# Pinning the VectorE and ScalarE order of a trunk's last projection, and moving two weight tiles and a low-rank half

## The chip, the cores and the metric

One core of one Trainium2 chip runs the whole program. The time is the device time of one execution in microseconds (us). A program of this kind has five engines that run their own instruction lists in parallel (TensorE, VectorE, ScalarE, GpSimd and SyncE, in the profile PE, DVE, ACT, POOL and SP) and wait for each other by semaphores. Most transfers here are issued by SP.

## The reference, cut to what matters

Two layers of a streaming encoder run over 4096 prompt frames and 32 sample frames of width 1024. Layer 0 splits one input projection into a convolution branch and a gated linear recurrence; layer 1 pools trailing frames. Each layer adds its gated output to the stream, and a final RMSNorm follows:

```python
        h = rms_norm(x, norm_g[l]) * (1.0 + scale[:, None, :]) + shift[:, None, :]
        if l % 2 == 0:
            y, cb, gs = even_mixer(h, ...)
        else:
            y, pb = pool_mixer(h, ...)
        x = x + gate[:, None, :] * y
    return rms_norm(x, final_g), ...
```

Two pieces of it matter here. In `even_mixer` the value columns v and 16 low-rank columns lr come out of the same projection, and the forget gate is made from lr: `log_a = log_sigmoid(lr @ gate_w2 + gate_b) / 16`. In `pool_mixer` the last line is the last projection, `(p * scale * silu(gate)) @ w_out`, a product of 4128 rows by 1024 with a 1024 by 1024 matrix.

## The kernel before, in words

All products are float32 products in three passes: each operand is split into a high and a low part, and high by high, high by low and low by high are summed in PSUM. ScalarE writes the high part of an operand, VectorE subtracts it from the source and writes the low part. For a weight tile `split_w` does this (lines 116 to 119), one ScalarE and one VectorE instruction of 128x1024 per tile, from a staging buffer into which SP has loaded it. There are two such staging buffers (tag `st`), so the load of a tile waits for the split of the tile two before it.

The rows go in 11 blocks, ten of 384 rows and a last one of 256 prompt and 32 sample rows, through these stages:

- Stage A makes the convolution branch's projections, stage C the first layer's output projection, stage D the second layer's input projection and pooling. They are touched by the change only through `split_w`, which issues the same instructions there.
- Stage B, the recurrence branch (lines 874 to 1020). Its loop over blocks interleaves the projection of the block at hand with the attention of the block before. A tile of 128 rows makes its v and lr columns in two halves (`v_unit`, line 874, PSUM names `psv`): half 0 is 264 columns of v, half 1 the other 248 and the 16 lr columns (`lrt`). When all tiles are done, VectorE splits lr (`lrs`, lines 930 and 932), TensorE transposes it (`pslr`, line 936), ScalarE evacuates it (`lrT`), TensorE makes the first gate column tile (`psg`) and then the forget gate (`psz`). The attention pieces of the block before are the calls pa, pk, pu, po and pt: scores (`psat`), key transposes and state update (`psku`), output (`pso`), and the transposes of the normalized output (`psoT`, from `on`, line 845). The last block also loads and splits eight weight tiles of stage C (`w_c`).
- Stage E, the last projection (from line 1327). It takes the prompt rows in 16 pairs of 128-row tiles. A pair is a 2 by 2 block product done with Strassen's and Winograd's seven products. The left operands are the quarters y of two tiles and their combinations S1 to S4 (`comb`, line 1370); `make(i)` (lines 1373 to 1385) splits the operand of product i into `op`, ScalarE first, VectorE behind it. The right operands are 14 weight tiles, `w_e` 0 to 13, of which product i uses 2i and 2i+1. Each product is 12 matmuls of 128x512. The products go in turn into three PSUM banks, and after each one VectorE adds the bank to the residual rows `xE` (`add`, line 1441). Bank 0 serves products 0, 2, 4 and 6, so product 2 can't start before the add behind product 0 has read it, and so on. The rows of the first tile are complete after product 5, those of the second after product 6. Then `finish` (lines 1396 to 1404) squares and sums them on ScalarE (`junkE`), makes 1/rms on GpSimd in two instructions (`rt_E`, `rE`), scales on VectorE (`SCALAR_TENSOR_TENSOR`, line 1403) and stores the tile. `make(i)` for the next pair follows each add.
- Behind the 16 pairs come the sample rows with eight more weight tiles (`load_S`, `w_s` 0 to 7, split in the last pair) in two products `psES`, and their own norm.

The order of the work: a scheduler sets each engine's list, except where `tc.keep_in_program_order` ties an instruction to the source's order. In stages B to E only TensorE is tied (`PIN["on"]`). In stage E, VectorE, ScalarE and SP are in the scheduler's order. `load_E(0)` to `load_E(11)` stand in the last block of stage D (line 1322), `load_E(12)` and `load_E(13)` in stage E behind `make(3)` (line 1418).

Of the kernel before, what the change touches and what calls it, by code (L numbers as in the profile page):

```python
# [8 lines left out]
F32 = mybir.dt.float32  # L9
# [3 lines left out]
AF = mybir.ActivationFunctionType  # L13
ALU = mybir.AluOpType
# [16 lines left out]
def trunk(  # L31
# [8 lines left out]
    nc = tc.nc  # L40
# [8 lines left out]
    while L - s0 > TB - NS:  # L49
        b = Blk()  # L50
# [65 lines left out]
    def split_w(w, st, nk, n):  # L116

        nc.scalar.activation(w[:, 0], st, AF.Copy)  # L118
        nc.vector.tensor_tensor(out=w[:, 1], in0=st, in1=w[:, 0].bitcast(F32), op=ALU.subtract)  # L119

# [37 lines left out]
    PASS = ((0, 0), (0, 1), (1, 0))  # L158
    PIN = {"on": False, "act": False}

# [572 lines left out]
    with ExitStack() as bctx:  # L733
# [169 lines left out]
        for blk in blocks:  # L903
# [17 lines left out]
            v_unit(blk, hs, vt, lrt, 1, 1)  # L921
            pk(2), pt(0)
            v_unit(blk, hs, vt, lrt, 2, 0)
            pu(2), po(2)
            v_unit(blk, hs, vt, lrt, 2, 1)
            pt(1)

# [334 lines left out]
    with tc.tile_pool(name="D", bufs=2, reuse_waits="tile") as dp:  # L1262
# [3 lines left out]
        for blk in blocks:  # L1266
# [3 lines left out]
            for idx, (kind, j) in enumerate(dord):  # L1270
# [45 lines left out]
                if blk.last:  # L1316

                    if idx < 8:
                        rv_load(idx)
                    if 2 <= idx < 10:  # L1320
                        rv_gemm(idx - 2, hs)
                    if 1 <= idx < 13:
                        load_E(idx - 1, halves=idx <= 8)
# [3 lines left out]
    with tc.tile_pool(name="E", bufs=2, reuse_waits="tile") as ep:  # L1327
        PIN["on"] = True

# [30 lines left out]
        class Left:  # L1360
# [7 lines left out]
            def comb(self, out, a, b, op):  # L1368
                t = ep.tile([P, 4, P], F32, tag="S", name=f"{out}_{self.p}", bufs=4)
                nc.vector.tensor_tensor(out=t, in0=self.A[a], in1=self.A[b], op=op)  # L1370
                self.A[out] = t

            def make(self, i):
                if i == 2:
                    self.comb("S1", "A21", "A22", ALU.add)
                    self.comb("S2", "S1", "A11", ALU.subtract)
                if i == 4:
                    self.comb("S3", "A11", "A21", ALU.subtract)
                if i == 5:
                    self.comb("S4", "A12", "S2", ALU.subtract)  # L1380
                src = self.A[("A11", "A12", "S2", "S1", "S3", "S4", "A22")[i]]
                o = ep.tile([P, 2, 4, P], F32R, tag="op", name=f"op{self.p}_{i}", bufs=8)
                nc.scalar.activation(o[:, 0], src, AF.Copy)  # L1383
                nc.vector.tensor_tensor(out=o[:, 1], in0=src, in1=o[:, 0].bitcast(F32), op=ALU.subtract)  # L1384
                self.ops[i] = o
# [10 lines left out]
        def finish(xt, n, name, dst):  # L1396
            junk = ep.tile([P, D], BF16, tag="junk", name=f"junk{name}", bufs=1)
            ss = sm.tile([P, 1], F32, tag="ss", name=f"ss{name}")
            nc.scalar.activation(junk[:n], xt[:n], AF.Square, accum_out=ss[:n])
            r = sm.tile([P, 1], F32, tag="r", name=f"r{name}")  # L1400
            rstd_pool(r[:n], ss[:n], n, 1, 1.0 / D, name)
            yield
            nc.vector.scalar_tensor_tensor(out=xt[:n], in0=xt[:n], scalar=r[:n], in1=fg[:n], op0=ALU.mult, op1=ALU.mult)
            nc.sync.dma_start(dst, xt[:n])
# [10 lines left out]
        for i in range(7):  # L1415
            cur.make(i)
            if i == 3:
                load_E(12, ep), load_E(13, ep)
                nc.sync.dma_start(fg, final_g.partition_broadcast(P))
# [14 lines left out]
        for p in range(len(pairs)):  # L1434
# [5 lines left out]
            def add(x, h, ps):  # L1440
                nc.vector.tensor_tensor(out=x[:, H[h]], in0=ps, in1=x[:, H[h]], op=ALU.add)  # L1441

# [75 lines left out]
```

## Time and profile before

| what | value |
|---|---|
| runs | 2895.23, 2896.0 and 2900.14 us, median 2896.0 us |
| the profiled execution | 2898.6 us, its span 2896.9 us |
| mean clock granted to TensorE | 0.993 of full speed |
| TensorE busy | 2819.6 us, 97% of the span |
| VectorE busy | 1964.5 us, 68% |
| ScalarE busy | 1031.9 us, 36% |
| GpSimd busy | 243.8 us, 8% |

The span is the time between the first and the last recorded work of the core; the execution's own time is measured outside of it and is 1.7 us longer. Busy times are averages over stages with different limits, and a share of 97% says only that TensorE is the engine that nearly everything waits for: a microsecond can be won where TensorE stands still or runs at its lower clock.

### The profile page before, as it was taken

To read this page: it belongs to the slowest core of one execution; us is meant where nothing else is said; L and a number is where in the kernel's file an instruction comes from. 1 tells how busy PE (TensorE), PEld (TensorE's weight loads), DVE (VectorE), ACT (ScalarE), POOL (GpSimd) and SP (SyncE) were. 2 spreads that over 40 slices of the span, in tenths; PEclk is the share of its full clock that TensorE was granted. 3 is DMA by queue.
4 is the path that set the end of the run, shared out by engine and by line. 5 is a ranking of instruction groups with operands and counts; after the bars stand their busy time and mean duration, and the time that the engine had idled before them with its cause. 6 is when DMAs were issued, how large, how long until landed. Compare 5 with 4: busy or idle time off the path is not lost. (4 is left out here: it accounts for less than half of the span.)

```text
span 2896.9 us, 43268 instructions
## 1 busy us (share of the span) xinstructions
PE 2819.6 (97%) x16593; PEld 2613.4 (90%) x16593; DVE 1964.5 (68%) x3907; ACT 1031.9 (36%) x2137; POOL 243.8 (8%) x492
## 2 busy tenths in 40 slices
PE   7999999999999999998999999999999999999998
PEld 5999999998999999997878888999999999977776
DVE  4997886888788888885866675533333333587766
ACT  4434334334344333333232224422322322433333
POOL 1110000000000000001111110011111110000000
PEclk9999999999999999999999999999999999999999
DMA  8422322242211111115455554322222221464544
GB/s 287 155 86 104 110 104 91 79 120 75 61 52 45 45 51 59 38 55 173 164 197 184 194 196 139 112 68 71 70 69 68 71 68 51 150 205 147 167 145 145
DMA packets 249666, 323.69 MB, mean 112 GB/s; under 512 B 18793, under 2 KB 198907, under 8 KB 248947
## 3 DMA queue, kind: packets, MB, share of 16 engines
q1 hardware_dynamic: 248635, 318.78, 33.9%
q8 instruction: 130, 2.13, 0.3%
q0 software_dynamic: 704, 2.11, 0.2%
q14 instruction: 77, 0.63, 0.1%
q10 hardware_dynamic: 120, 0.04, 0.0%
HBM read 211.21 MB, written 109.65 MB: 111 GB/s over the span
## 5 line engine op out<-in xcount | busy, mean ns | idle before, releaser
L162 PE MATMUL psC<-w_c,hC 128*128 128x512 f32 (+1 forms) x1568 | 377.9, 398 | 0.0
L162 PE MATMUL psD<-h,w_du 128*128 128x384 f32 (+1 forms) x2112 | 376.6, 332 | 0.1
L162 PE MATMUL psD<-h,w_dg 128*128 128x384 f32 (+1 forms) x2112 | 376.4, 332 | 0.0
L413 DVE SCALAR_TENSOR_TENSOR co<-g,cwt,co 128x384 f32<-128x384 f32 (+1 forms) x660 | 370.1, 606 | 4.9
L162 PEld LDWEIGHTS psD<-h,w_du 128*128 128x128 f32 x2112 | 357.8, 188 | 0.9 <-DVE h L152 0.4
L162 PEld LDWEIGHTS psD<-h,w_dg 128*128 128x128 f32 x2112 | 357.8, 188 | 0.4
L162 PEld LDWEIGHTS psC<-w_c,hC 128*128 128x128 f32 (+1 forms) x1568 | 293.6, 190 | 60.8
L413 DVE SCALAR_TENSOR_TENSOR coB<-glB,cwt,coB 128x384 f32<-128x384 f32 x600 | 333.8, 614 | 0.0
L162 PE MATMUL psE<-w_e,op 128*128 128x512 f32 x1344 | 310.7, 392 | 18.5 <-DVE xE L1441 13.9
L162 PEld LDWEIGHTS psE<-w_e,op 128*128 128x128 f32 x1344 | 252.0, 189 | 77.1 <-ACT op L1383 21.6
L162 PE MATMUL psv<-w_wv,hB 128*128 128x264 f32 (+1 forms) x1568 | 207.8, 288 | 2.1 <-ACT vt L887 2.1
L162 PEld LDWEIGHTS psv<-w_wv,hB 128*128 128x128 f32 (+1 forms) x1568 | 194.9, 187 | 6.4 <-ACT vt L887 2.5
L162 PE MATMUL psA<-h,w_aglu 128*128 128x384 f32 (+1 forms) x1056 | 191.9, 335 | 0.4 <-ACT h L172 0.2
L162 PE MATMUL psg<-hB,w_bg 128*128 128x384 f32 (+1 forms) x1056 | 190.8, 338 | 1.4 <-DVE xn L708 1.4
L162 PE MATMUL psA<-h,w_aval 128*128 128x384 f32 (+1 forms) x1056 | 189.1, 333 | 0.0
L162 PE MATMUL psA<-h,w_agate 128*128 128x384 f32 (+1 forms) x1056 | 187.2, 333 | 0.0
L162 PEld LDWEIGHTS psg<-hB,w_bg 128*128 128x128 f32 x1056 | 182.7, 192 | 2.1 <-issue 1.6
L1290 DVE COPY halo<-u 128x15 f32<-128x15 f32 x80 | 14.2, 178 | 250.7 <-ACT u L1286 250.7
L162 PEld LDWEIGHTS psA<-h,w_aglu 128*128 128x128 f32 x1056 | 180.4, 189 | 2.8 <-issue 1.7
L162 PEld LDWEIGHTS psA<-h,w_aval 128*128 128x128 f32 x1056 | 178.4, 188 | 0.1
L162 PEld LDWEIGHTS psA<-h,w_agate 128*128 128x128 f32 x1056 | 178.0, 188 | 0.1
L1311 DVE SCALAR_TENSOR_TENSOR sgD<-p,gbs,sgD 128x384 f32<-128x384 f32 (+1 forms) x96 | 56.1, 591 | 125.4 <-ACT sgD L1307 124.0
(268 smaller groups left out, 3719.1 us busy)
## 6 DMA issues: line engine op xcount, KB each, us to landing
x<-in_x_prompt SPq DMA_DIRECT2D x64, 512.0 KB
aw<-in_ada_w SPq DMA_DIRECT2D x32, 512.0 KB
x1D<-x SPq DMA_DIRECT2D x32, 512.0 KB
x<-x1D SPq DMA_DIRECT2D x32, 512.0 KB
out<-xE SPq DMA_DIRECT2D x32, 512.0 KB
hfD<-hf_a SPq DMA_DIRECT2D x80, 192.0 KB
hfB<-hfD SPq DMA_DIRECT2D x40, 384.0 KB
y1D<-sgD SPq DMA_DIRECT2D x80, 192.0 KB
```

The costliest lines, as they stand in the source:

```text
L162: ins = nc.tensor.matmul(*args, **kw)
L413: nc.vector.scalar_tensor_tensor(out=out[:, :w], in0=src[:, j:j + w], scalar=cwt[:, c, j:j + 1], in1=out[:, :w], op0=ALU.mult, op1=ALU.add)
L1290: nc.vector.tensor_copy(halo[:, j, :], u[:, TB:TB + PP])
L1311: nc.vector.scalar_tensor_tensor(out=y1[:, c0:c0 + m], in0=pt[:, a:a + m], scalar=gbs[:, j:j + 1], in1=sgt[:, c0:c0 + m], op0=ALU.add, op1 ...
```

## The change

It has four parts. ScalarE's and VectorE's instructions of stage E are tied to the source's order, as TensorE's are: the splits, combinations, adds and the two ends of `finish`. `load_E(10)` and `load_E(11)` move from the last block of stage D to behind `make(1)` of the first pair in stage E. In stage B the third tile's half 1 (with the lr columns) is made before its half 0, and ahead of the state update `pu(2)` and the transposes `pt(0)`. Outside of stage E the new `pin` and `act` do nothing, as the flags are off there.

```diff
@@ -115,8 +115,8 @@
 
     def split_w(w, st, nk, n):
 
-        nc.scalar.activation(w[:, 0], st, AF.Copy)
-        nc.vector.tensor_tensor(out=w[:, 1], in0=st, in1=w[:, 0].bitcast(F32), op=ALU.subtract)
+        act(w[:, 0], st, AF.Copy)
+        pin(nc.vector.tensor_tensor(out=w[:, 1], in0=st, in1=w[:, 0].bitcast(F32), op=ALU.subtract))
 
     def wslot(name):
         return wp.tile([P, SLOT], F32R, tag="w", name=name)
@@ -156,7 +156,11 @@
         return h
 
     PASS = ((0, 0), (0, 1), (1, 0))
-    PIN = {"on": False, "act": False}
+    PIN = {"on": False, "act": False, "dve": False}
+
+    def pin(ins):
+        if PIN["dve"]:
+            tc.keep_in_program_order(ins)
 
     def mmul(*args, **kw):
         ins = nc.tensor.matmul(*args, **kw)
@@ -919,11 +923,11 @@
             v_unit(blk, hs, vt, lrt, 1, 0)
             pu(1), po(1), pa(2)
             v_unit(blk, hs, vt, lrt, 1, 1)
-            pk(2), pt(0)
+            pk(2)
+            v_unit(blk, hs, vt, lrt, 2, 1)
+            pu(2), pt(0)
             v_unit(blk, hs, vt, lrt, 2, 0)
-            pu(2), po(2)
-            v_unit(blk, hs, vt, lrt, 2, 1)
-            pt(1)
+            po(2), pt(1)
 
             lrs = bp.tile([P, 2 * P], F32R, tag="kA", name=f"lrs{blk.i}")[:, 0:144].rearrange("p (i a b) -> p i a b", i=3, a=3)
             for (i0, i1, m) in ([(0, nsub, P)] if not blk.last else [(i, i + 1, sb[1]) for i, sb in enumerate(blk.subs)]):
@@ -1319,13 +1323,13 @@
                         rv_load(idx)
                     if 2 <= idx < 10:
                         rv_gemm(idx - 2, hs)
-                    if 1 <= idx < 13:
+                    if 1 <= idx < 11:
                         load_E(idx - 1, halves=idx <= 8)
             hs = nxt
     hctx.close()
 
     with tc.tile_pool(name="E", bufs=2, reuse_waits="tile") as ep:
-        PIN["on"] = True
+        PIN["on"] = PIN["act"] = PIN["dve"] = True
 
         ep.tile([P, D], F32, tag="x", name="x_first", bufs=4)
         ep.tile([P, 2048], F32R, tag="we", name="we_first", bufs=2)
@@ -1367,7 +1371,7 @@
 
             def comb(self, out, a, b, op):
                 t = ep.tile([P, 4, P], F32, tag="S", name=f"{out}_{self.p}", bufs=4)
-                nc.vector.tensor_tensor(out=t, in0=self.A[a], in1=self.A[b], op=op)
+                pin(nc.vector.tensor_tensor(out=t, in0=self.A[a], in1=self.A[b], op=op))
                 self.A[out] = t
 
             def make(self, i):
@@ -1380,8 +1384,8 @@
                     self.comb("S4", "A12", "S2", ALU.subtract)
                 src = self.A[("A11", "A12", "S2", "S1", "S3", "S4", "A22")[i]]
                 o = ep.tile([P, 2, 4, P], F32R, tag="op", name=f"op{self.p}_{i}", bufs=8)
-                nc.scalar.activation(o[:, 0], src, AF.Copy)
-                nc.vector.tensor_tensor(out=o[:, 1], in0=src, in1=o[:, 0].bitcast(F32), op=ALU.subtract)
+                act(o[:, 0], src, AF.Copy)
+                pin(nc.vector.tensor_tensor(out=o[:, 1], in0=src, in1=o[:, 0].bitcast(F32), op=ALU.subtract))
                 self.ops[i] = o
 
         def prod(ps, left, i, first):
@@ -1396,11 +1400,11 @@
         def finish(xt, n, name, dst):
             junk = ep.tile([P, D], BF16, tag="junk", name=f"junk{name}", bufs=1)
             ss = sm.tile([P, 1], F32, tag="ss", name=f"ss{name}")
-            nc.scalar.activation(junk[:n], xt[:n], AF.Square, accum_out=ss[:n])
+            act(junk[:n], xt[:n], AF.Square, accum_out=ss[:n])
             r = sm.tile([P, 1], F32, tag="r", name=f"r{name}")
             rstd_pool(r[:n], ss[:n], n, 1, 1.0 / D, name)
             yield
-            nc.vector.scalar_tensor_tensor(out=xt[:n], in0=xt[:n], scalar=r[:n], in1=fg[:n], op0=ALU.mult, op1=ALU.mult)
+            pin(nc.vector.scalar_tensor_tensor(out=xt[:n], in0=xt[:n], scalar=r[:n], in1=fg[:n], op0=ALU.mult, op1=ALU.mult))
             nc.sync.dma_start(dst, xt[:n])
 
         ends = []
@@ -1414,6 +1418,8 @@
         cur, xs = Left(0), load_xE(0)
         for i in range(7):
             cur.make(i)
+            if i == 1:
+                load_E(10), load_E(11)
             if i == 3:
                 load_E(12, ep), load_E(13, ep)
                 nc.sync.dma_start(fg, final_g.partition_broadcast(P))
@@ -1438,7 +1444,7 @@
             bank = [mm([P, 512], f"psE{p}_{q}") for q in range(3)]
 
             def add(x, h, ps):
-                nc.vector.tensor_tensor(out=x[:, H[h]], in0=ps, in1=x[:, H[h]], op=ALU.add)
+                pin(nc.vector.tensor_tensor(out=x[:, H[h]], in0=ps, in1=x[:, H[h]], op=ALU.add))
 
 
             for i, (q, first, adds) in enumerate(((0, 1, (x1, 0)), (1, 1, (x1, 0)), (0, 0, (x1, 1)), (2, 1, (x2, 1)),
```

Where instructions moved, first on VectorE at the start of stage E, behind the last instruction of stage D. `w_e` are low parts of weight tiles, `op0_i` those of pair 0's operands (pair number, then product), `S1_0` to `S4_0` its combinations. Before:

```order
L119 TENSOR_TENSOR w_e12_25319<-st_e12_25320,w_e12_25319 128x1024
L119 TENSOR_TENSOR w_e13_25324<-st_e13_25325,w_e13_25324 128x1024
L1384 TENSOR_TENSOR op0_0_25303<-y0_0_25295,op0_0_25303 128x512
L1384 TENSOR_TENSOR op0_1_25306<-y0_0_25295,op0_1_25306 128x512
L1370 TENSOR_TENSOR S1_0_25309<-y0_1_25297 128x512
L1370 TENSOR_TENSOR S2_0_25311<-S1_0_25309,y0_0_25295 128x512
L1370 TENSOR_TENSOR S3_0_25330<-y0_0_25295,y0_1_25297 128x512
L1370 TENSOR_TENSOR S4_0_25335<-y0_0_25295,S2_0_25311 128x512
L1384 TENSOR_TENSOR op0_2_25313<-S2_0_25311,op0_2_25313 128x512
L1384 TENSOR_TENSOR op0_3_25316<-S1_0_25309,op0_3_25316 128x512
L1384 TENSOR_TENSOR op0_4_25332<-S3_0_25330,op0_4_25332 128x512
L1384 TENSOR_TENSOR op0_5_25337<-S4_0_25335,op0_5_25337 128x512
```

With the change:

```order
L1388 TENSOR_TENSOR op0_0_25293<-y0_0_25285,op0_0_25293 128x512
L1388 TENSOR_TENSOR op0_1_25296<-y0_0_25285,op0_1_25296 128x512
L119 TENSOR_TENSOR w_e10_25299<-st_e10_25300,w_e10_25299 128x1024
L119 TENSOR_TENSOR w_e11_25304<-st_e11_25305,w_e11_25304 128x1024
L1374 TENSOR_TENSOR S1_0_25309<-y0_1_25287 128x512
L1374 TENSOR_TENSOR S2_0_25311<-S1_0_25309,y0_0_25285 128x512
L1388 TENSOR_TENSOR op0_2_25313<-S2_0_25311,op0_2_25313 128x512
L1388 TENSOR_TENSOR op0_3_25316<-S1_0_25309,op0_3_25316 128x512
L119 TENSOR_TENSOR w_e12_25319<-st_e12_25320,w_e12_25319 128x1024
L119 TENSOR_TENSOR w_e13_25324<-st_e13_25325,w_e13_25324 128x1024
L1374 TENSOR_TENSOR S3_0_25330<-y0_0_25285,y0_1_25287 128x512
L1388 TENSOR_TENSOR op0_4_25332<-S3_0_25330,op0_4_25332 128x512
```

The splits of tiles 12 and 13 stood ahead of the first operands; now tiles 10 and 11 (that were split in stage D) stand behind the first two operands, tiles 12 and 13 behind the fourth, and S3 and S4 behind them.

VectorE again, in a pair in mid-stage, from the add behind product 5 of pair 3 (`xE3_0<-psE3_2`) on. The add into `xE3_1` is that behind product 6, the adds into `xE4_0` are the first two of pair 4. Before:

```order
L1441 TENSOR_TENSOR xE3_0_25643<-psE3_2_25798,xE3_0_25643 128x512
L1384 TENSOR_TENSOR op4_6_25934<-y4_1_25790,op4_6_25934 128x512
L1403 SCALAR_TENSOR_TENSOR xE3_0_25643<-xE3_0_25643,rE3_0_25903,fg_25292 128x1024
L1441 TENSOR_TENSOR xE3_1_25645<-psE3_0_25796,xE3_1_25645 128x512
L1384 TENSOR_TENSOR op5_0_25963<-y5_0_25937,op5_0_25963 128x512
L1403 SCALAR_TENSOR_TENSOR xE3_1_25645<-xE3_1_25645,rE3_1_25930,fg_25292 128x1024
L1441 TENSOR_TENSOR xE4_0_25792<-psE4_0_25945,xE4_0_25792 128x512
L1384 TENSOR_TENSOR op5_1_25979<-y5_0_25937,op5_1_25979 128x512
L1441 TENSOR_TENSOR xE4_0_25792<-psE4_1_25946,xE4_0_25792 128x512
```

With the change:

```order
L1447 TENSOR_TENSOR xE3_0_25643<-psE3_2_25798,xE3_0_25643 128x512
L1374 TENSOR_TENSOR S4_4_25907<-y4_0_25788,S2_4_25848 128x512
L1388 TENSOR_TENSOR op4_5_25909<-S4_4_25907,op4_5_25909 128x512
L1447 TENSOR_TENSOR xE3_1_25645<-psE3_0_25796,xE3_1_25645 128x512
L1407 SCALAR_TENSOR_TENSOR xE3_0_25643<-xE3_0_25643,rE3_0_25903,fg_25282 128x1024
L1388 TENSOR_TENSOR op4_6_25934<-y4_1_25790,op4_6_25934 128x512
L1447 TENSOR_TENSOR xE4_0_25792<-psE4_0_25945,xE4_0_25792 128x512
L1407 SCALAR_TENSOR_TENSOR xE3_1_25645<-xE3_1_25645,rE3_1_25930,fg_25282 128x1024
L1388 TENSOR_TENSOR op5_0_25963<-y5_0_25937,op5_0_25963 128x512
L1447 TENSOR_TENSOR xE4_0_25792<-psE4_1_25946,xE4_0_25792 128x512
L1388 TENSOR_TENSOR op5_1_25979<-y5_0_25937,op5_1_25979 128x512
```

The scale of a tile's rows now has one or two more instructions between it and the add whose sum it waits for, and S4 and the operand of product 5, which were made earlier, now follow the add behind product 5.

ScalarE in stage B, last block (`psv10_2x` is its third tile, x the half; `9_2` names pieces of the block before). Before:

```order
L783 ACTIVATE kA9_2_13615<-psku9_2_13612 128x256
L206 ACTIVATE vt10_2_13406<-psv10_20_13628 32x264
L838 ACTIVATE junkB9_2_13664,ss49_2_13663<-pso9_20_13653 128x128 x2
L838 ACTIVATE junkB9_2_13664,ss49_2_13663<-pso9_21_13654 128x128
L118 ACTIVATE w_c00_14281<-st_c00_14279 128x1024
L838 ACTIVATE junkB9_2_13664,ss49_2_13663<-pso9_21_13654 128x128
L118 ACTIVATE w_c01_14286<-st_c01_14284 128x1024
L206 ACTIVATE lrt10_13407<-psv10_21_13676 32x16
L206 ACTIVATE vt10_2_13406<-psv10_21_13676 32x248
```

With the change:

```order
L787 ACTIVATE kA9_2_13615<-psku9_2_13612 128x256
L210 ACTIVATE lrt10_13407<-psv10_21_13620 32x16
L210 ACTIVATE vt10_2_13406<-psv10_21_13620 32x248
L176 ACTIVATE w_c00_14281<-st_c00_14279 128x1024
L176 ACTIVATE w_c01_14286<-st_c01_14284 128x1024
L210 ACTIVATE vt10_2_13406<-psv10_20_13655 32x264
L842 ACTIVATE junkB9_2_13685,ss49_2_13684<-pso9_20_13674 128x128 x2
L842 ACTIVATE junkB9_2_13685,ss49_2_13684<-pso9_21_13675 128x128
```

`lrt` moved ahead of the two weight splits and of the squares (`junkB`), which end with the tile's other half behind them.

## Rows read from the trace of the kernel before

**Rows 1.** Waits of TensorE by line and releaser: total us, times, longest us

```profile
PE psE L162 <- DVE xE L1441: 13.9, 15, 1.1
...
PE pslr L167 <- DVE lrs L932: 12.2, 11, 5.0
```

**Rows 2.** Timeline of TensorE in stage E: start us, us, instruction, count, [idle before <- releaser]

```profile
2602.51 19.32 PE L162 MATMUL psE<-w_e,op 128*128 128x512 f32 x84 [0.94 <-DVE xE L1441]
...
2622.85 19.32 PE L162 MATMUL psE<-w_e,op 128*128 128x512 f32 x84 [1.02 <-DVE xE L1441]
...
2846.69 30.20 PE L162 MATMUL psE<-w_e,op 128*128 128x512 f32 x132 [1.11 <-DVE xE L1441]
...
2877.30 3.01 PE L162 MATMUL psE<-w_e,op 128*128 128x512 f32 x12 [0.41 <-DVE xE L1441]
```

**Rows 3.** Timeline of all engines, stage E, end of a pair

```profile
2610.99 0.69 DVE L1441 TENSOR_TENSOR xE<-psE,xE 128x512 f32<-128x512 f32 x1 [0.63 <-PE psE L162]
...
2613.70 0.69 DVE L1441 TENSOR_TENSOR xE<-psE,xE 128x512 f32<-128x512 f32 x1 [0.64 <-PE psE L162]
...
2614.57 1.06 ACT L1399 ACTIVATE junkE<-xE 128x1024 bf16<-128x1024 f32 x1 [0.23 <-DVE xE L1441]
...
2616.08 0.55 POOL L213 TENSOR_TENSOR rE<-rt_E,mhalf 128x1 f32<-128x1 f32 x1
...
2616.42 0.63 ACT L1383 ACTIVATE op<-y 128x512 fp32r<-128x512 f32 x1 [0.71 <-PE psE L162]
...
2616.66 1.29 DVE L1403 SCALAR_TENSOR_TENSOR xE<-xE,rE,fg 128x1024 f32<-128x1024 f32 x1 [1.60 <-POOL rE L213]
...
2617.87 0.68 DVE L1441 TENSOR_TENSOR xE<-psE,xE 128x512 f32<-128x512 f32 x1
...
2618.47 0.68 DVE L1384 TENSOR_TENSOR op<-y,op 128x512 fp32r<-128x512 f32 x1
...
2620.82 1.29 DVE L1403 SCALAR_TENSOR_TENSOR xE<-xE,rE,fg 128x1024 f32<-128x1024 f32 x1 [1.67 <-POOL rE L213]
...
2622.02 0.68 DVE L1441 TENSOR_TENSOR xE<-psE,xE 128x512 f32<-128x512 f32 x1
```

**Rows 4.** Timelines of SP, ScalarE, TensorE and VectorE around the start of stage E

```profile
2537.73 0.32 SPq L1229 DMA_DIRECT2D st_e<-wED  x1
...
2543.04 1.06 ACT L118 ACTIVATE w_e<-st_e 128x1024 fp32r<-128x1024 f32 x1 [4.88 <-DMA st_e<-wED]
...
2547.70 3.32 PE L162 MATMUL psD<-h,w_dg 128*128 128x288 f32 x24
...
2552.81 0.65 DVE L1311 SCALAR_TENSOR_TENSOR sgD<-p,gbs,sgD 128x256 f32<-128x256 f32 x2
...
2553.37 2.35 DVE L119 TENSOR_TENSOR w_e<-st_e,w_e 128x1024 fp32r<-128x1024 f32 x2
...
2556.38 6.65 PE L162 MATMUL psE<-w_e,op 128*128 128x512 f32 x22 [1.66 <-DVE op L1384]
...
2563.22 38.34 PE L162 MATMUL psE<-w_e,op 128*128 128x512 f32 x168 [0.19 <-DVE xE L1441]
```

**Rows 5.** Windows: length, busy us of PE, PEld, DVE, ACT, POOL, then clock, DMA share, GB/s

```profile
2556.00:2561.00 5.00, 4.62 (x14) 3.76 (x15) 4.96 (x9) 2.71 (x6) 0.00 (x0) 0.67 1.00 290
```

**Rows 6.** Timelines of TensorE and VectorE in stage B, blocks 0, 1 and last

```profile
665.54 0.80 PE L167 MATMUL pslr<-ident,lrs 128*48 128x128 f32 x3 [3.36 <-DVE lrs L932]
...
730.18 0.49 PE L167 MATMUL pslr<-ident,lrs 128*48 128x128 f32 x3 [0.43 <-DVE lrs L932]
...
1308.34 0.24 PE L167 MATMUL pslr<-ident,lrs 32*48 32x32 f32 x1 [5.00 <-DVE lrs L932]
...
1308.52 5.63 PE L162 MATMUL psg<-hB,w_bg 128*128 128x288 f32 x24
...
1330.44 1.23 DVE L119 TENSOR_TENSOR w_c<-st_c,w_c 128x1024 fp32r<-128x1024 f32 x1 [1.99 <-ACT w_c L118]
...
1332.09 0.33 PE L167 MATMUL psku<-ident,Ek 128*128 128x128 f32 x1 [3.20 <-DVE Ek L1013]
```

## The prediction

> **What bounds the kernel now.** I read the waits of TensorE first, since an engine that is busy 97% of the span can only be helped where it stands still. The reader is to see two totals: 13.9 us in 15 waits for VectorE's adds in stage E, and 12.2 us in 11 waits for the low-rank split in stage B [rows 1]. Next the timeline of TensorE in stage E: every pair begins its product 2 behind a gap of about 1 us, from 2602.51 to 2846.69, thirteen gaps and twelve periods [rows 2]. A period is thus 244.18 / 12 = 20.35 us. A pair without a gap would take seven products of the 2.71 us that lie between two adds released by TensorE [rows 3], 19.0 us; so each pair loses 1.3 us. Then the timeline of all engines across one such gap [rows 3]: the add behind product 5 is at 2613.70, the square behind it at 2614.57, 1/rms at 2616.08, and VectorE stands idle for 1.60 us until the scale at 2616.66. Only then come the add behind product 6, an operand, another idle 1.67 us before the second scale, and at last, at 2622.02, the add that TensorE needs. The bound is VectorE's queue order, not its work. Third, the start of stage E [rows 4, 5] and four places of stage B [rows 6].
>
> **The change part by part.**
>
> *Stage E in mid-stage.* No instruction is added; the order is new. Let the add behind product 5 start at 0. The square starts at 0.87 and takes 1.06, and 1/rms is ready at 2.93 (2616.08 + 0.55 - 2613.70) [rows 3]. VectorE meanwhile does S4 (priced like an add, 0.60 from start to start by the pair of rows at 2617.87 and 2618.47), then waits for ScalarE's high part of operand 5, which now stands behind the square: square and read-out until about 2.1, 0.63 for the part [rows 3], so VectorE's part is 2.8 to 3.4. The add behind product 6 follows until 4.1. The scale finds 1/rms ready and takes 1.21 (2616.66 to 2617.87), until 5.2. The second square runs from 4.3 to 5.5 beside it, ScalarE's part of operand 6 until 6.2, VectorE's until 6.9, and the next pair's first add until 7.5. Product 1 of that pair ends at 3 x 2.71 = 8.1. So the gap closes with 0.6 us to spare, and the second scale waits for GpSimd behind the add that matters. VectorE is not the new bound: 18 instructions of 0.6 and two of 1.2 are 13.2 us of 19. Thirteen gaps of 1.3 are -17.0. One other place is as tight: behind the add of product 4 stand S3 and the hand-over for operand 4 before the add of product 5, worked out as 0.69 + 0.6 + 0.63 + 0.68 and some 0.3 of hand-overs, 2.9 against 2.71. I leave 0.1 us a pair for it and take **-15.7**; bounds -17.0 and, if half of the gap comes back, -8.5.
>
> *The start of stage E.* TensorE ends stage D at 2551.02 (2547.70 + 3.32) and begins product 2 at 2563.22 [rows 4]. VectorE is free at 2553.46. It will then do two operands (to 2554.7), two weight splits that take 2.35 together (to 2557.1), two combinations (2558.3) and, over ScalarE's part, operands 2 and 3 (2560.3). The split of tile 12 comes next, but its load waits for a staging buffer that is free when tile 10 is split, about 2555.9. A load of this kind was issued at 2537.73 and read at 2543.04, 5.3 us [rows 4]. Ahead of it on SP now stand the final gain and two residual tiles, three times 512 KB, at the 290 GB/s of this stretch [rows 5] 5.4 us from about 2553.9. Either way tile 12 lands at about 2561.2, tile 13 between 2562.4 and 2564. Behind it ScalarE's split takes 1.06 [rows 4] and VectorE's 1.2, to about 2565.5. All of VectorE's and ScalarE's queue stands behind these two: S3, operand 4, S4, operands 5 and 6, some 4.2 us with their hand-overs, and behind them the first add, 0.69. Product 2 starts at about 2570.4, **7.2 us later**. That products 0 and 1 start 2.2 us earlier (their operand's low part at 2554.2 and no longer at 2556.38) buys nothing, as product 2 waits in any case. TensorE will have stood idle for some 9 us; after the idle time at 2551 it was granted 0.67 of full speed in the window 2556 to 2561, the lower of its two levels (1.2 of 2.4 GHz) for part of it [rows 5], and 22 matmuls took 6.65 us [rows 4] where 22 of 0.226 (2.71 / 12) are 5.0. I add 1.8 for that: **+9**, bounds +5 (the loads land in 3.5 us and the clock holds) and +14 (tile 13 comes 3 us later still, and the lower clock lasts twice as long).
>
> The Trainium skill, "DMA: Bandwidth & Descriptors", section "Anatomy of one DMA", gives a transfer a fixed 2.0 us and its bytes at 436 GB/s. By that, 512 KB would be an estimated 3.2 us where the row has 5.3, product 2 would come about 2 us earlier, and the sum would be 2876 in place of the figure below; the row and the 290 GB/s decide here.
>
> *The last pair.* Its gap of 0.41 [rows 2] goes. The split of weight tile 5 for the sample rows is now queued behind the first square, and those of tiles 6 and 7 behind the second, with VectorE's halves in front of or behind the last adds. Two squares with their read-outs are 2.5 us; the second `psES` product waits for tile 7. **+2.3** with the bounds 0 (the transfer of tile 7 is later than that anyway) and +5.
>
> *Stage B.* With half 1 made first, a whole half lies between `lrt` and `pslr`. In blocks 1 to 9 the wait is 0.43 each [rows 6], **-3.9**. What is late next there: the transposes of the third `on`, which now have less TensorE work ahead of them; by the rows of block 1 there is still more than a microsecond to spare, so I take nothing off. Block 0 waits 3.36 [rows 6], partly because ScalarE's evacuations come late behind loads; I take **-1.5**, bounds 0 and -3.4. The last block waits 5.00, then runs `psg` in 5.63 us, where 24 matmuls of that shape take 3.32 at the end of stage D [rows 4]: 2.3 us of lower clock that go with the idle time. Later a split of a stage C tile at 1330.44 waits on VectorE ahead of `Ek` and costs TensorE 3.20; it moves behind `Ek`. Together 10.5, of which I take **-8**, since the splits still wait for their loads on the same ScalarE queue that makes the gates; bounds -3 and -10.5.
>
> **The sum.** -15.7 + 9 - 0.4 + 2.3 - 3.9 - 1.5 - 8 = -18.2. The profiled execution took 2898.6, 2.6 above the median of the runs; against the median of 2896.0 the forecast is **2878**. All terms at their good ends give -30, 2866.
>
> **The rivals.** *The gap only moves (no change).* If a hand-over between ScalarE and VectorE costs 0.2 more than I worked out, the chain of operand 4 makes the add behind product 5 late, the 0.6 us to spare are gone, and product 2 waits as long as before: -18.2 + 15.7 is -2.5, 2893. For it: VectorE and ScalarE now hand over four times where work was made ahead. Against it: nearly 6 of VectorE's 19 us are free. 12%.
>
> *The pinned queue stalls product 2 for longer than before (slower).* The place is the same add; the mechanism is that both waits for 1/rms, 1.60 and 1.67 [rows 3], stay in front of it in a queue in which nothing may overtake. The chain would be 7.5 + 3.2 = 10.7 against 8.1, a gap of 2.6 a pair in place of 1.3: 13 x 2.5 instead of the -15.7 and its 0.1s, 2909. It decides from a gap of 1.9. Against it: 1/rms is ready at 2.93 and wanted at 4.1, and the second scale stands behind the add. 5%.
>
> *The start of stage E costs double.* Tile 13's load crawls behind the residual tiles and pair 1's loads, and product 2 comes 18 us later: 2887, still faster. 9%.
>
> *The last block of stage B gives nothing.* The next wait (a stage C tile's load, 1/rms of the recurrence's output) takes the place of each one removed, and block 0 stays as it is: 2888. 10%.
>
> That the change doesn't do what it says is no rival: the lists of VectorE and ScalarE show each move.
>
> **How the numbers follow.** The forecast has the remaining 64%, with the bounds of its terms mostly inside 2866 to 2890. The range 2866 to 2893 takes in the two smaller-gain cases and half of the first rival. A measurement of this kernel can tell about 0.2%, 5.8 us, from no change: faster is 64 + 9 + 10 = 83%, same 12%, slower 5%.
>
> **What would show it.** In the changed profile the gaps in front of product 2 are gone and the period is 19.0 to 19.2 us; TensorE stands idle once for 8 to 12 us before product 2 of pair 0, with ScalarE's split of tile 12 or 13 waiting for a load; the waits of `pslr` in blocks 1 to 9 are gone and the last block's `psg` takes about 3.4 us. A period above 20 us, or scales that still wait in front of the adds, would make it wrong; so would a start of stage E that is no later than before.

## The result, and the profile after

The changed kernel takes 2879.39 us in the median of 4 runs (2878.16 to 2880.98), against 2895.98 (4 runs) before: 16.6 us less. The ratio is 0.994 with a 95% interval of 0.9923 to 0.9957, faster by more than 0.2%. The forecast was 2878 with a range of 2866 to 2893. The profiled execution took 2878.16 us, its span 2876.5 us, with a mean granted clock of 0.992.

In the waits of TensorE (line and releaser, total us, times, longest us) the two totals the prediction began with [rows 1] look like this:

```profile
PE psE L166 <- DVE xE L1447: 14.2, 1, 14.2
...
PE psku L171 <- DVE Ek L1017: 2.7, 1, 2.7
...
PE pslr L171 <- DVE lrs L936: 0.5, 1, 0.5
```

Fifteen small waits for the adds of stage E have become one of 14.2 us. Of eleven waits for the low-rank split one is left, in block 0, and the wait for `Ek` has not gone.

The windows of 240 us in mid-stage (length, busy us of PE, PEld, DVE, ACT, POOL, then clock, DMA share, GB/s), changed kernel:

```profile
2545.00:2550.00 5.00, 0.00 (x0) 0.00 (x0) 1.94 (x2) 2.11 (x2) 0.00 (x0) 0.51 0.29 118
...
2555.00:2560.00 5.00, 4.16 (x12) 3.40 (x13) 2.50 (x5) 0.33 (x1) 0.00 (x0) 0.62 0.69 199
...
2600.00:2840.00 240.00, 240.00 (x1061) 198.78 (x1060) 174.75 (x252) 78.55 (x140) 18.48 (x50) 1.00 0.51 163
```

The same long window of the kernel before:

```profile
2600.00:2840.00 240.00, 227.79 (x992) 184.92 (x992) 170.00 (x237) 77.14 (x129) 17.05 (x47) 1.00 0.47 154
```

TensorE is busy for all of the 240 us where it had stood idle for 12.2. The two short windows are from the start of the stage and are read below.

The timeline of all engines at the end of a pair, with the change, answers to [rows 3]:

```profile
2606.49 0.69 DVE L1447 TENSOR_TENSOR xE<-psE,xE 128x512 f32<-128x512 f32 x1
...
2607.36 1.06 ACT L176 ACTIVATE junkE<-xE 128x1024 bf16<-128x1024 f32 x1 [1.56 <-DVE xE L1447]
...
2608.87 0.55 POOL L217 TENSOR_TENSOR rE<-rt_E,mhalf 128x1 f32<-128x1 f32 x1
...
2609.06 0.69 DVE L1388 TENSOR_TENSOR op<-S,op 128x512 fp32r<-128x512 f32 x1 [1.27 <-ACT op L176]
...
2609.67 0.69 DVE L1447 TENSOR_TENSOR xE<-psE,xE 128x512 f32<-128x512 f32 x1
...
2610.27 1.28 DVE L1407 SCALAR_TENSOR_TENSOR xE<-xE,rE,fg 128x1024 f32<-128x1024 f32 x1
...
2612.23 0.69 DVE L1388 TENSOR_TENSOR op<-y,op 128x512 fp32r<-128x512 f32 x1 [0.69 <-ACT op L176]
...
2612.84 0.68 DVE L1447 TENSOR_TENSOR xE<-psE,xE 128x512 f32<-128x512 f32 x1
...
2613.44 1.28 DVE L1407 SCALAR_TENSOR_TENSOR xE<-xE,rE,fg 128x1024 f32<-128x1024 f32 x1
```

From the add behind product 5 at 2606.49 to the next pair's first add at 2612.84 are 6.35 us, where before they were 8.32. The scale at 2610.27 finds 1/rms ready (2608.87 + 0.55) and has no idle time in front of it, and the second scale stands behind the add.

TensorE at the start of stage E, which answers to [rows 4]:

```profile
2531.18 3.32 PE L166 MATMUL psD<-h,w_dg 128*128 128x288 f32 x24
...
2535.57 6.04 PE L166 MATMUL psE<-w_e,op 128*128 128x512 f32 x24 [1.07 <-ACT op L176]
...
2555.84 144.45 PE L166 MATMUL psE<-w_e,op 128*128 128x512 f32 x630 [14.23 <-DVE xE L1447]
```

Product 2 starts 21.34 us after stage D's end (2531.18 + 3.32); before it was 12.20. What it waits for is in the timeline of the other engines:

```profile
2535.60 1.29 DVE L1388 TENSOR_TENSOR op<-y,op 128x512 fp32r<-128x512 f32 x2
...
2538.27 1.46 SPq L1233 DMA_DIRECT2D st_e<-wED  x2
...
2546.95 1.06 ACT L176 ACTIVATE w_e<-st_e 128x1024 fp32r<-128x1024 f32 x1 [5.05 <-DMA st_e<-wED]
...
2548.03 2.48 DVE L119 TENSOR_TENSOR w_e<-st_e,w_e 128x1024 fp32r<-128x1024 f32 x2 [5.34 <-ACT w_e L176]
...
2555.01 0.69 DVE L1447 TENSOR_TENSOR xE<-psE,xE 128x512 f32<-128x512 f32 x1
...
2560.26 0.69 DVE L1447 TENSOR_TENSOR xE<-psE,xE 128x512 f32<-128x512 f32 x1 [2.76 <-PE psE L166]
```

The loads of tiles 12 and 13 are issued from 2538.27 on, and ScalarE can read tile 12 at 2546.95, 8.7 us later. VectorE stands idle for 5.34 us in front of the splits, and the add that TensorE needs comes at 2555.01.

TensorE at the end of the program:

```profile
2856.55 5.72 PE L166 MATMUL psES<-w_s,hS 128*96 128x512 f32 x24
...
2862.48 0.47 PE L166 MATMUL psES<-w_s,hS 128*96 128x512 f32 x1 [0.22 <-ACT w_s L176]
...
2863.74 2.08 PE L166 MATMUL psES<-w_s,hS 128*96 128x512 f32 x7 [0.79 <-DVE w_s L119]
```

The second half of the sample rows' product now waits twice for a split weight tile; from the first `psES` matmul to the end of the span are 19.95 us, before 16.75.

Stage B, TensorE in blocks 0 and 1:

```profile
662.79 0.49 PE L171 MATMUL pslr<-ident,lrs 128*48 128x128 f32 x3 [0.49 <-DVE lrs L936]
...
727.45 0.49 PE L171 MATMUL pslr<-ident,lrs 128*48 128x128 f32 x3
```

And in the last block, TensorE and VectorE:

```profile
1295.12 3.42 PE L166 MATMUL psg<-hB,w_bg 128*128 128x288 f32 x24
...
1314.40 1.23 DVE L119 TENSOR_TENSOR w_c<-st_c,w_c 128x1024 fp32r<-128x1024 f32 x1 [1.72 <-ACT w_c L176]
...
1316.05 0.33 PE L171 MATMUL psku<-ident,Ek 128*128 128x128 f32 x1 [2.68 <-DVE Ek L1017]
```

The wait in block 1 is gone, that of block 0 fell from 3.36 to 0.49, and the last block's `psg` takes 3.42 us and not 5.63 [rows 6].

A ledger of all that, as differences of start times in the timelines of TensorE: stage B from its first `psv` to the first matmul of stage C, stage C to the first matmul of stage D, stage D to its last group of 24 matmuls, from that group's start to product 2, from product 2 to the first `psES` matmul, and from there to the end of the span. The rows e1 to e9 are the experiments of the next section, "again" is the changed kernel in a second series. All us:

| kernel | stage B | C | D | to product 2 | product 2 to psES | tail |
|---|---|---|---|---|---|---|
| before | 720.6 | 432.8 | 752.8 | 15.5 | 316.9 | 16.8 |
| the change | 705.3 | 433.0 | 750.6 | 24.7 | 300.7 | 20.0 |
| the change, again | 707.3 | 433.7 | 751.5 | 24.4 | 302.0 | 19.6 |
| e1, no swap | 720.7 | 431.3 | 751.9 | 24.5 | 301.5 | 20.2 |
| e2, swap only | 704.1 | 433.8 | 752.8 | | | 16.7 |
| e3, tiles 10, 11 in D | 706.6 | 431.4 | 751.8 | 17.9 | 301.1 | 20.2 |
| e4, ScalarE tied | 704.4 | 432.9 | 752.1 | 12.3 | 308.6 | 18.5 |
| e5, VectorE tied | 704.1 | 430.9 | 751.4 | 24.6 | 301.6 | 17.5 |
| e6, loads first | 703.7 | 433.5 | 751.0 | 21.2 | 302.4 | 19.2 |
| e7, tail free | 705.3 | 433.1 | 751.8 | 24.1 | 301.8 | 17.6 |
| e9, scale first | 706.7 | 435.8 | 751.6 | 24.4 | 329.4 | 20.3 |
| e8, both late | 707.5 | 430.6 | 751.2 | 12.4 | 301.5 | 17.5 |

(For e2 the timeline joins product 2 to the groups around it.) For the change the columns are -15.3, +0.2, -2.2, +9.1, -16.2 and +3.2; with 0.7 us more before stage B the sum is -20.4, the difference of the two spans (2876.5 - 2896.9). The two profiled executions lie 2.6 above and 1.2 below their medians, which is the rest to 16.6.

### The profile page after: what moved, and what is told of

Its sections match the earlier page's. It is cut to its first block, busy times and chain, and to the rows that moved or that the text cites. A ratio compares the mean times of both kernels' runs of the same rounds, so it can differ in the third digit from the quotient of the medians.

```text
span 2876.5 us, 43290 instructions
## 1 busy us (share of the span) xinstructions
PE 2813.8 (98%) x16593; PEld 2612.0 (91%) x16593; DVE 1959.3 (68%) x3907; ACT 1023.1 (36%) x2137; POOL 243.6 (8%) x492
## 4 chain that ended last, share of the span: by engine, by line
PE 81%; issue 10%; DMA 3%; DVE 3%; POOL 2%; ACT 1%; SPq 0%; POOLq 0%; ACTq 0%; DVEq 0%
PE psD L166 25%; PE psA L166 18%; PE psC L166 9%; PE psv L166 6%; PE psg L166 6%; PE psq L166 3%; PE psk L166 3%; PE pso L166 2%; PE pst_d L171 1%; PE psE L166 1%; PE ps_wo L166 1%; PE pst_a L171 1%; PE psku L166 1%; PE psoT L171 1%; DMA aw<-in_ada_w 1%
## 5 line engine op out<-in xcount | busy, mean ns | idle before, releaser
L166 PE MATMUL psE<-w_e,op 128*128 128x512 f32 x1344 | 306.9, 391 | 15.3 <-DVE xE L1447 14.2
L1294 DVE COPY halo<-u 128x15 f32<-128x15 f32 x80 | 14.2, 178 | 253.3 <-ACT u L1290 253.3
```

Source lines behind the costliest of these rows:

```text
L166: ins = nc.tensor.matmul(*args, **kw)
L1294: nc.vector.tensor_copy(halo[:, j, :], u[:, TB:TB + PP])
```

## The experiments

Times are medians with their ratio to the kernel before in the same series, and its 95% interval.

**Stage B alone, taken away and put in.** e1 undoes the swap:

```diff
-            pk(2)
-            v_unit(blk, hs, vt, lrt, 2, 1)
-            pu(2), pt(0)
-            v_unit(blk, hs, vt, lrt, 2, 0)
-            po(2), pt(1)
+            pk(2), pt(0)
+            v_unit(blk, hs, vt, lrt, 2, 0)
+            pu(2), po(2)
+            v_unit(blk, hs, vt, lrt, 2, 1)
+            pt(1)
```

> The changed kernel with the third tile's two halves in stage B back in their old order; stage E as changed. Theory (the parts add up, each at its place in the trace): the changed kernel reaches the first product of stage C 14.6 us earlier than before, all of it won in stage B, so without the swap this run takes 2879.4 + 14.6 = 2894. The 2 us that the last block of stage D gained stay, as they belong to the weight tiles that left it. Rival (what stage B wins is taken back later, by stage C's loads): 2880 to 2887. The transposes' waits for the low-rank split come back at 11 places, some 12 us in total.

Measured: 2892.93 us, 0.9988 (0.9979 to 0.9997). The waits of TensorE have the old row again:

```profile
PE pslr L171 <- DVE lrs L936: 12.1, 11, 5.0
```

e2 makes the same edit the other way round in the kernel before, as its only change.

> The kernel before with only the swap of the third tile's halves. Theory: 2896.0 - 14.6 = 2881.4; stage E keeps its thirteen gaps of about 1 us. With e1 the two parts sum to the whole: swap -14.6, rest -2. Rival (the forecast's own price of 13.4 with the stage C loads taking some back): 2883 to 2889.

Measured: 2881.69, 0.9952 (0.9935 to 0.9968). Both came within about 1 us of the first theory: the swap is worth some 14 us of the 16.6, by either road, and nothing of it is taken back later. All the rest of the change, its largest term among it, is together worth 2 to 4. Stage D is another matter. e1's expectation gave its 2 us to the two tiles that left it; e3 and e8 have them back in stage D and take 751.8 and 751.2 there, no more than the runs without them, so that falls. The kernels with stage E unpinned, before and e2, are at 752.8. About half of the difference between before and the change are waits that vary from run to run: in stage D's last block the products `psrv` wait for split weight tiles `w_r`, 1.1 us in three waits before, 1.0 us in two with e4, and not at all in the change. The rest stays open. (The tie of TensorE's instructions does not reach into stage D: line 1177 of the kernel before takes it off at the end of stage C, and line 1328 sets it again in stage E. The order there is the scheduler's; TensorE's is nevertheless the same in all these runs.)

**Which engine's order closes the gap.** e4 and e5 tie only one of the two:

```diff
-        PIN["on"] = PIN["act"] = PIN["dve"] = True
+        PIN["on"] = PIN["act"] = True      # e4
+        PIN["on"] = PIN["dve"] = True      # e5
```

> The changed kernel with only ScalarE tied to the source's order in stage E, VectorE left to the scheduler. Its VectorE list puts the scale of a pair's second tile behind the first add of the next pair, as the pinned list does, but the first two adds of pair 0 ahead of the splits of weight tiles 12 and 13. Theory A (the gap came from the second scale standing ahead of the add, and the start's stall from the two splits that wait for their loads ahead of the add): no gaps in mid-stage, and product 2 starts 9 to 12 us after stage D's end and not 21.3, so 2868 to 2873. Theory B (all of VectorE's list has to be pinned): the gaps of 1.3 us return, 13 of them, 2879 + 17 - 10 = 2886 or more.

> The changed kernel with only VectorE tied in stage E, ScalarE left to the scheduler; the high parts of weight tiles 10 and 11 are then made in stage D. VectorE's list is that of the changed kernel. Theory (VectorE's order alone decides both the gaps and the start): no gaps, product 2 some 21 us after stage D's end, 2877 to 2881. Rival (the order of ScalarE, the square ahead of the operand, closes the gap): gaps return, 2890 or more.

Measured: e4 2872.39, 0.9915 (0.99 to 0.9931); e5 2874.49, 0.9928 (0.9913 to 0.9943). Either alone closes the gap, and both medians lie below that of the change, though the intervals overlap. TensorE of e4:

```profile
2544.49 5.68 PE L166 MATMUL psE<-w_e,op 128*128 128x512 f32 x24 [1.89 <-DVE xE L1447]
...
2553.57 81.26 PE L166 MATMUL psE<-w_e,op 128*128 128x512 f32 x348 [3.39 <-DVE xE L1447]
...
2635.17 153.63 PE L166 MATMUL psE<-w_e,op 128*128 128x512 f32 x672 [0.34 <-DVE xE L1447]
```

Product 2 starts 9 us after stage D's end. The two splits still wait for their loads, but now behind the first two adds, and TensorE pays 3.39 us for them two products later. In mid-stage only three gaps of 0.3 to 0.8 are left. VectorE of e4 at the end of a pair:

```profile
2602.22 1.28 DVE L1407 SCALAR_TENSOR_TENSOR xE<-xE,rE,fg 128x1024 f32<-128x1024 f32 x1 [2.26 <-POOL rE L217]
...
2604.03 0.69 DVE L1447 TENSOR_TENSOR xE<-psE,xE 128x512 f32<-128x512 f32 x1
...
2605.23 0.69 DVE L1447 TENSOR_TENSOR xE<-psE,xE 128x512 f32<-128x512 f32 x1
...
2606.98 1.28 DVE L1407 SCALAR_TENSOR_TENSOR xE<-xE,rE,fg 128x1024 f32<-128x1024 f32 x1 [1.06 <-POOL rE L217]
```

The first scale still stands ahead of the add behind product 6, as before the change, and VectorE idles 2.26 us for it. Only the second has moved behind the next pair's first add (2605.23). That is what e4, e5 and the change share; in the list before, it stood ahead. An operand has moved behind the second scale too; e9, below, moves nothing but scales. In both runs tiles 10 and 11 have left stage D too. No run has that move with neither engine tied, so it isn't shown that the pin, and not this move, made the scheduler's list better; e3 below shows that the two pins close the gap without the move. e5 came out 2.5 us below its expectation, at the tail (17.5 us and not 20.0): with ScalarE free, the last two splits of the sample rows' tiles go ahead of the second square.

**The scale in front of the add.** e9 keeps everything pinned and swaps two lines:

```diff
                 prod(bank[q], cur, i, first)
-                add(*adds, bank[q])
                 flush()
+                add(*adds, bank[q])
```

> The changed kernel with, in the pinned order, each scale of finished rows ahead of the next product's add, and not behind it: the second scale then stands ahead of the first add of the next pair, as it did before the change. Nothing is added or left out. Theory (what decides is whether the wait for 1/rms stands ahead of the add that TensorE waits for): the gap comes back larger than before, since operand 6 now waits for the second square as well: add at about 10.0 after the add behind product 5 where product 1 ends at 8.1, some 1.9 us at 14 or 15 pairs, 2905 to 2909. Rival (the slack of VectorE absorbs it): 2879 to 2885.

Measured: 2907.41, 1.0033 (1.0023 to 1.0044), slower than before. TensorE has a gap at each pair again:

```profile
2601.97 19.32 PE L166 MATMUL psE<-w_e,op 128*128 128x512 f32 x84 [1.36 <-DVE xE L1447]
...
2622.75 19.32 PE L166 MATMUL psE<-w_e,op 128*128 128x512 f32 x84 [1.45 <-DVE xE L1447]
```

The period is 20.78 us, 1.7 above the 19.04 of a pair without a gap. The timeline shows the chain:

```profile
2613.18 0.69 DVE L1447 TENSOR_TENSOR xE<-psE,xE 128x512 f32<-128x512 f32 x1
...
2618.41 1.06 ACT L176 ACTIVATE junkE<-xE 128x1024 bf16<-128x1024 f32 x1 [2.69 <-DVE xE L1447]
...
2620.72 1.28 DVE L1407 SCALAR_TENSOR_TENSOR xE<-xE,rE,fg 128x1024 f32<-128x1024 f32 x1
...
2621.92 0.68 DVE L1447 TENSOR_TENSOR xE<-psE,xE 128x512 f32<-128x512 f32 x1
```

From the add behind product 5 at 2613.18 to the next pair's first add at 2621.92 are 8.74 us, against 6.35 in the change. The expectation had 10.0, so the size of the chain was overstated and the time was met nevertheless. e9 moves both scales of a pair by one place, and that is worth 26 to 28 us of this kernel (against 2881.44 and 2879.39); e4, where the first scale keeps its old place and the gap is all but gone, says that the gap hangs on the second. It is nearly the slower rival of the prediction made real, with a chain of 8.74 where the rival had 10.7.

**What makes the start of stage E late.** e3 leaves tiles 10 and 11 in stage D:

```diff
-                    if 1 <= idx < 11:
+                    if 1 <= idx < 13:
...
-            if i == 1:
-                load_E(10), load_E(11)
```

> The changed kernel with weight tiles 10 and 11 split in the last block of stage D again, as before; order pinned, tiles 12 and 13 still behind the fourth operand. Their staging buffers are then free early and both loads land before stage D ends. Theory (the stall at the start of stage E is the wait for these two loads, 5.1 us on ScalarE, plus the two splits of 2.4 us that leave the list): product 2 starts 13 to 14 us after stage D's end and not 21.3; stage D's last block takes 1 to 2 us more; 2872 to 2874. Rival (the loads compete with the other traffic wherever they stand, or the chain of hand-overs alone makes the stall): less than 3 us gained, 2877 or more.

Measured: 2872.93, 0.9917 (0.9901 to 0.9934). ScalarE and TensorE:

```profile
2540.84 1.99 ACT L176 ACTIVATE w_e<-st_e 128x1024 fp32r<-128x1024 f32 x2
...
2549.60 10.63 PE L166 MATMUL psE<-w_e,op 128*128 128x512 f32 x38 [6.46 <-DVE xE L1445]
```

The splits of tiles 12 and 13 wait for nothing, and product 2 starts 14.5 us after stage D's end. Its theory had 13 to 14, and the time is within what it gave. The two tiles' move is thus a loss of some 6.5 us by itself. e6 leaves them and puts the two loads ahead of the other traffic on SP:

```diff
-            nc.sync.dma_start(st, src)
+            ld = nc.sync.dma_start(st, src)
+            if pool is not None:
+                tc.keep_in_program_order(ld)
...
-                (nc.sync if p else nc.gpsimd).dma_start(xt, x1D[b.i][i])
+                ld = (nc.sync if p else nc.gpsimd).dma_start(xt, x1D[b.i][i])
+                if p == 1:
+                    tc.keep_in_program_order(ld)
...
-                nc.sync.dma_start(fg, final_g.partition_broadcast(P))
...
+        tc.keep_in_program_order(nc.sync.dma_start(fg, final_g.partition_broadcast(P)))
         wS = {}
```

> The changed kernel with SP's order tied so that the loads of weight tiles 12 and 13 stand ahead of those of pair 1's residual tiles and of the final gain, which stood ahead of them (1.5 MB). Theory (the 8.7 us from the issue of tile 12's load to its use are queueing behind that traffic; alone it takes 5.3 as in stage D): tile 12 is used 3 us earlier, product 2 starts 3 us earlier, 2876 to 2877. Rival (the load takes that long whatever stands ahead): 2879 to 2880.

Measured: 2875.53, 0.9929 (0.9914 to 0.9944). SP, ScalarE and TensorE:

```profile
2536.20 1.46 SPq L1233 DMA_DIRECT2D st_e<-wED  x2
...
2540.23 1.06 ACT L176 ACTIVATE w_e<-st_e 128x1024 fp32r<-128x1024 f32 x1 [0.40 <-issue]
...
2550.29 6.19 PE L166 MATMUL psE<-w_e,op 128*128 128x512 f32 x14 [10.77 <-DVE xE L1451]
```

The load now takes at most 4.0 us from issue to use (the 0.40 us that ScalarE stands idle in front of it are not put down to the load) and not 8.7, and product 2 comes 3.5 us earlier: the queue of 1.5 MB in front of it was the price.

**The tail.** e7 frees both engines in the last pair:

```diff
                 if not more and i == 2:
+                    PIN["act"] = PIN["dve"] = False
```

> The changed kernel with VectorE and ScalarE left to the scheduler again from the middle of the last pair on. Theory (the last pair's pinned order, with the splits of the sample rows' weight tiles 5 to 7 behind the squares, makes the end 3.2 us longer than before): the stretch from the first psES matmul to the end is 16.8 to 17.5 us and not 19.95; 2876 to 2877. Rival (the tail is set by the weight loads): no change, 2879 to 2880.

Measured: 2878.39, 0.9936 (0.9921 to 0.9951). TensorE:

```profile
2856.46 6.88 PE L166 MATMUL psES<-w_s,hS 128*96 128x512 f32 x29
...
2863.72 0.94 PE L166 MATMUL psES<-w_s,hS 128*96 128x512 f32 x3 [0.38 <-DVE w_s L119]
```

The tail is 17.6 us, 2.3 less than with the change, as expected, but the median lies between the two expectations, 1.0 below the change here and 3.0 below it in its second series, where the change itself moved by 2. The trace shows the mechanism; the time alone does not prove it.

**A better version.** e8 puts the findings together:

```diff
-                    if 1 <= idx < 11:
+                    if 1 <= idx < 13:
...
-        for i in range(7):
+        for i in range(4):
             cur.make(i)
             if i == 1:
-                load_E(10), load_E(11)
-            if i == 3:
                 load_E(12, ep), load_E(13, ep)
-                nc.sync.dma_start(fg, final_g.partition_broadcast(P))
...
+            if p == 0:
+                tc.keep_in_program_order(nc.sync.dma_start(fg, final_g.partition_broadcast(P)))
...
                 add(*adds, bank[q])
                 flush()
+                if p == 0 and i < 3:
+                    cur.make(4 + i)
...
                 if not more and i == 2:
+                    PIN["act"] = PIN["dve"] = False
```

Besides, the loads of pair 1's `y` and `xE` are tied in that order on SP, with the lines of e6.

> A version put together from what the runs showed. The changed kernel, but: weight tiles 10 and 11 split in stage D as before (e3); tiles 12 and 13 split right behind the first two operands, their loads long done; pair 0's operands 4, 5 and 6 made in the pair's loop, behind the adds of products 0, 1 and 2, so that the first add stands ahead of them; SP's order tied so that pair 1's left operands are loaded ahead of its residual tiles and the gain (e6); VectorE and ScalarE left free from the middle of the last pair (e7). Theory (the stall at the start is what stands ahead of the first add in VectorE's queue): e3's product 2 started 14.5 us after stage D's end; S3, S4 and three operands with their hand-overs, 4.6 us, leave that list, so 9 to 10 us; the tail is 2 us shorter: 2865 to 2868. Rival (the work only moves behind the add, and products 4 to 6 wait for it): 2871 to 2874.

> The changed kernel itself, unedited, beside e8 on the same chip, to compare the two in one series: 2878 to 2881. Both theories expect the same; it shows how far runs of one kernel lie apart.

Measured in one series: e8 2866.05, 0.9891 (0.9876 to 0.9906); the change again 2881.44, 0.9948 (0.9935 to 0.9962). e8 is 15.4 us faster than the change and 29.9 faster than before. TensorE of e8:

```profile
2540.93 5.72 PE L166 MATMUL psE<-w_e,op 128*128 128x512 f32 x24 [1.60 <-DVE xE L1450]
...
2547.32 2.99 PE L166 MATMUL psE<-w_e,op 128*128 128x512 f32 x12 [0.66 <-DVE xE L1450]
...
2551.32 48.98 PE L166 MATMUL psE<-w_e,op 128*128 128x512 f32 x215 [1.02 <-DVE xE L1450]
```

Product 2 starts 9.1 us after stage D's end, and of the rival's waits for products 4 and 5 there are 0.66 and 1.02 us. The change itself came out 2 us higher than in its first series, 0.4 above what was expected, and in the ledger its stages differ by up to 2 us from those of the first series. That is the measure for small differences here.

## Why the prediction was right, point by point

The forecast's sum was -18.2; the medians moved by -16.6 and the two spans by -20.4. Its direction, its two largest gains and its one large loss are as it had them, with these sizes. That the sum came so close is in part luck: single terms were off by 1 to 2 us in both directions, and 2.2 us of stage D were not in it.

- *Mid-stage, -15.7 and -0.4 for the last pair.* The stretch from product 2 to `psES` shrank by 16.2 us, and that includes 1.5 of lower clock at its start, so the gaps gave 17.7 where 16.1 was taken. Not a single gap is left, and the period is 19.04. The chain was put at 7.5 us between the two adds and takes 6.35; the 0.1 us a pair that the prediction kept back for the other tight place was not needed. e4 and e9 show that the reason is the right one.
- *Start of stage E, +7.2 and 1.8 for the clock.* Measured +9.1, and 1.5 for the clock: in the window 2555 to 2560 TensorE is busy for 4.16 us with the 12 matmuls of product 2, which take 2.72 from product to product later (4.21 here, and 5.26 in the second series). TensorE stood idle for 14.23 us, more than the 8 to 12 named as a sign. The granted clock was 0.51 in the window 2545 to 2550, while TensorE did nothing, 0.62 from 2555 to 2560, and 1.00 from 2560 on: the lower level, 1.2 GHz, and then 2.4. The term that was too small is the load of tile 12, put at 5.3 us from a row of stage D and in fact 8.7. The prediction did see the 1.5 MB ahead of it, but took "either way" the same landing.
- *The rule against the row.* The Trainium skill, "DMA: Bandwidth & Descriptors", section "Anatomy of one DMA — SWDGE (gpsimd) path", would have an estimated 3.2 us for this load. Its fit is given for transfers that GpSimd issues, and SP issues this one, which the prediction passed over. With the queue ahead of it the load took 8.7, so the row decided in the right direction and not far enough; with the queue behind it, in e6, it took at most 4.0, and there the page is nearer than the row of 5.3. What a load issued by SP takes alone, no run here shows.
- *The last pair and the tail, +2.3.* Measured +3.2, and only about half by the mechanism named. The second `psES` product, with its waits for split tiles, takes 5.6 us where it took 3.9. The other 1.5 us come behind the last matmul, where the scale of the last prompt tile (2866.77) stands on VectorE ahead of the adds for the sample rows; this the prediction did not have.
- *Stage B, -13.4.* Measured -15.3, with other shares. From the first `psv` to block 0's second `psg`: -2.7 where -1.5 was taken. Blocks 1 to 9: -6.2 where nine waits of 0.43 are 3.9, so 0.69 a block. In block 1 the starts of the last `psoT` ahead of `pslr` and of `pslr` lie 0.49 apart, before 1.03: the wait cost 0.54, more than the 0.43 of idle time that the waits list shows; the other 0.15 stays open. The last block: -6.4 where -8 was taken. That its slow `psg` was the clock, as the prediction took it, holds: it was granted 0.50 from 1308 to 1311 before, and 1.00 in the change.
- *The step that failed* is inside that last term: the 3.20 us wait for `Ek` was to go, as its split moves behind `Ek`. The split ahead of that one took its place on VectorE, at 1314.40, waiting for ScalarE's part as the first did, and TensorE's wait is 2.68. The prediction looked at the one instruction that moved and not at the one behind which `Ek` now stood.
- *Stages C and D* were left out and moved by +0.2 and -2.2; the other runs put stage D's part at the level of their scatter.
- *A sum of a rival.* The start at double cost took 18 us against +9, which includes the clock; against the 7.2 of product 2 alone it gives 2889, not 2887.

Of the rivals, the gap that only moves and the pinned queue that stalls did not happen; the double cost of the start did not either. That stage B's last block gives nothing was wrong by 6 us.

## What to carry to other kernels

An engine's list costs what stands in front of the instruction that the bound engine waits for: ask for each such instruction which waiting one is ahead of it, and move that one behind it. The place of a pair's two scales against two adds decided 26 to 28 us here, and the second of them the gap, while the pinning of either engine closed it. When an order is pinned, look hardest at its two ends, where loads are young: a weight split that waits for its load needs its load issued before the stage, or a place behind the first adds.

## What was not expected

- Pinning one of the two engines was no worse than pinning both, by the medians better (2872.4 and 2874.5 against 2879.4 and 2881.4), although the full pinning leaves no gap in mid-stage.
- A 512 KB load of one tile took 8.7 us from issue to use with 1.5 MB ahead of it on SP's queue, at most 4.0 with that traffic behind it, and 5.3 in stage D before.
- Five lines of stage B gave some 14 us of the 16.6, since in stage E the gain in mid-stage and the loss at the start and the tail nearly cancel. TensorE's waits list shows 12.2 us for that releaser over all blocks; the lower clock behind the last block's wait, and 0.69 us gained in each of blocks 1 to 9 where 0.43 were idle, come on top.
